# Seven-product pairs of a ConvFFN: weight sums by adding transfers and VectorE, products reordered over four PSUM banks

## The chip, the cores and the metric

The kernel runs on one core of a Trainium2 chip, as one program of 25725 instructions. The metric is device time in microseconds (us), from the first to the last instruction of the slowest core, here the only one. The core has five engines with a queue each: TensorE (PE, matrix products; its weight loads are listed as PEld), VectorE (DVE), ScalarE (ACT), GpSimd (POOL) and SyncE (SP, which only issues DMAs here). POOL issues DMAs as well; those can add to what lies at their destination.

## The reference

One inference step of a two-layer decoder trunk over 544 tokens (512 of a prompt and 32 of eight samples), model width 1024. Layer 0 mixes tokens by causal pooling, layer 1 by a gated linear recurrence (HGRN2). Each layer ends with the same gated ConvFFN, and the change lies there:

```python
def conv_ffn(h, ctx, w_up, conv_w, conv_b, w_down):
    u = h @ w_up                                   # 1024 -> 2 x 2816
    full = jnp.concatenate([ctx, u], axis=1)
    c = conv_b + sum(full[:, j:j + L] * conv_w[j] for j in range(3))
    gate, val = jnp.split(c, 2, axis=-1)
    y = (jax.nn.gelu(gate, approximate=True) * val) @ w_down   # 2816 -> 1024
    return y, full[:, -2:]
```

All of it is in 32-bit floats. The kernel makes each product out of three faster ones: an operand is split into a rounded high part and the rest (`wh`, `wl` for weights, `xh`, `xl` for activations), and high times high, high times low and low times high are added in PSUM.

## The kernel before

**Tiling.** Activations lie transposed, 128 features by 544 tokens in a tile. `w_up` is cut into 44 blocks of 1024 by 128: 22 of the gate half, 22 of the value half. A pair is gate block j with value block j; its result is 2 x 128 features for 544 tokens. `w_down` is cut along its 2816 rows into five parts (`PARTS`, 6, 4, 4, 3 and 5 blocks of 128), and the output tiles of a part are made once its pairs are done.

**Two ways to make a pair.** The first six pairs of a layer (`SEVEN = PARTS[0]`) are made plainly, by `group` and `block`. The other 16 pairs, j = 6 to 21, are made by `seven(j)` with seven block products in place of eight (Strassen's scheme in Winograd's form): the four quarters are the two halves of the inner dimension by the two blocks of the pair for the weights, and by the two halves of the tokens (`U`, 272 each) for the activations. One product q is 4 k-tiles by 3 partial products, 12 matmuls of 272 columns. It needs sums of weight quarters (`seventh(i, q)`, once per pair) and sums of activation quarters (`operands(k, out)`, once per layer), and afterwards sums of the products on DVE and ACT (the list `after` in `seven`).

**Weight sums before.** `seventh` loads both 1024 by 128 blocks into two `raw` tiles A_ and B_ (512 KB each, three such buffers) and has POOL make three sums when q is 0 and a fourth when q is 6. `ensure_units` then turns each of the seven quarters into `wh` on ACT and `wl` on DVE, in the order of use, up to nine units ahead of the product (`ahead_units`). With the quarters named A.lo, A.hi, B.lo, B.hi the order of use is: sum, A.lo, sum, B.lo, A.hi, B.hi, sum.

**Products before.** Three banks per pair, out of four of the tag `pa`: Y, X, Z, and the seven products go to Y, X, Z, Y, X, Z, Y, of which the fifth and the seventh add to what the bank holds and the fourth and sixth start it anew, once its first value has been read.

**Activation sums.** `operands(k, out)` runs for k = 0 to 3 beside the pairs 4 and 5: two DVE multiplications by the norm's scale, four POOL subtractions of 272 columns, then a split by ACT and DVE (`both`). The results are the right-hand sides of all sixteen pairs.

**Order of the work.** Nothing is issued in program order. All operations are recorded (`Plan.record`) and `emit` makes a list schedule: an instruction's cost comes from `Plan.cost`, DMAs from a small model with a due time, tile buffers are handed out in their order, and each engine's queue is written out in the planned order of start. The engines then run these fixed queues in order, waiting on semaphores. Hence a number in `cost` can change the order on every engine in the whole kernel. `plan.hold` and `plan.after` give the operation recorded next an additional predecessor.

**Convolution buffers.** `new_u(j)` takes a buffer of the tag `t` (22 in all), has POOL clear two columns and copy 16 columns of context into it; DVE or ACT write the block's result beside it; `conv` then has POOL copy the new context out (`cv`, `pv`), ACT make the first tap and DVE the other two; `finish` adds the GELU on ACT and the product of gate and value on DVE, whose split results `yh`, `yl` the down products read.

**Order of pairs and down products.** `MIX` interleaves them: in part 1 the pairs are followed by 4, 4, 0 and 0 down products, in part 2 by 3, 3, 2 and 0, in part 3 by 3, 3 and 2, in part 4 by 2, 2, 2, 2 and 0.

Of the kernel before, what the change touches and what calls it, by code (L numbers as in the profile page):

```python
# [11 lines left out]
F32 = _mybir.dt.float32  # L12
F32R = _mybir.dt.float32r
I32 = _mybir.dt.int32
AF = _mybir.ActivationFunctionType
ALU = _mybir.AluOpType

P = 128
# [58 lines left out]
class Plan:  # L77
# [86 lines left out]
    def cost(eng, name, args, kw):  # L164
# [14 lines left out]
        if name == "dma_start":  # L179
            return 0.475 if eng == "SP" else 1.04  # L180
        ins = [a for a in list(args[1:]) + list(kw.values()) if hasattr(a, "shape")]
# [4 lines left out]
        if eng == "DVE":  # L186
            if name == "memset":
                return 0.01 + n / 960
            return 0.069 + n / (1920 if name == "tensor_scalar" and not psum else 960) + 0.06 * cols
        return 0.13 + n / 475  # L190

    def emit(self):
# [7 lines left out]
        for bufs, keys in self.tags.values():  # L200
            for q in range(bufs, len(keys)):
                extra[self.tiles[keys[q]][1][0]] += self.tiles[keys[q - bufs]][1]
        dma = lambda o: 2.0 + int(np.prod(o[3][0].shape)) * 4 / 359e3
        dur = [o[7] + (dma(o) if o[2] == "dma_start" else 0) for o in ops]
# [51 lines left out]
        for _ in range(n):  # L256
# [31 lines left out]
            if o[2] == "dma_start":  # L288
                st = max(at + o[7] + 0.65, dma_free)
                dma_free = st + dma(o) - 2.0  # L290
                end[i] = dma_free + 0.91
            else:
                end[i] = free[e]
# [52 lines left out]
def trunk_step(ctx: ExitStack, tc: _tile.TileContext, xT, xp, xs, spool, s0, fctx, par, gb0, cst, bands,  # L346
# [91 lines left out]
    raws, casts = {}, {}  # L438
    sums, mine = {}, {}

# [38 lines left out]
    def seventh(i, q):  # L479


        H = 4 * P
        if q == 0:
            raws[i] = A_, B_ = [wp.tile([P, KT * P], F32, tag="raw", name="raw") for _ in range(2)]
            for t, src in zip((A_, B_), stream[i][0]):
                SP.dma_start(t, src)

            mine[i] = dict(sums) or {q: tt((P, H)) for q in range(2)}
            POOL.tensor_tensor(mine[i][0], A_[:, 0:H], B_[:, 0:H], op=ALU.add)
            POOL.tensor_tensor(B_[:, 0:H], B_[:, 0:H], B_[:, H:2 * H], op=ALU.add)  # L490
            POOL.tensor_tensor(mine[i][1], B_[:, 0:H], A_[:, 0:H], op=ALU.add)
        A_, B_ = raws[i]
        if q == 6:
            POOL.tensor_tensor(A_[:, H:2 * H], A_[:, H:2 * H], mine[i][1], op=ALU.add)
        return (mine[i][1], A_[:, 0:H], mine[i][0], B_[:, 0:H], A_[:, H:2 * H], B_[:, H:2 * H], A_[:, H:2 * H])[q]

# [415 lines left out]
    def ffn(li, XH, XL, res, enter, mtag, leave, n_ahead, homes, hv=HV):  # L912
# [14 lines left out]

        def new_u(j):
            u = tt((P, UW))
            us = u[:, 2 + SEQ:UW].rearrange("p (b c) -> p b c", c=6)  # L930
            if li == 0 and j % NPAIR < 8:
                plan.hold(hx[1][64:64 + NS, :])
            POOL.memset(u[:, 0:2], 0.0)
            POOL.tensor_copy(us[:, :, 0:2], cv[:, j])
            return u, us
# [73 lines left out]
        def operands(k, out):  # L1009
# [3 lines left out]
            for z, f in ((za, k), (zb, k + 4)):  # L1013
                DVE.scalar_tensor_tensor(z, x_of(f), pcol(gn + f), R, op0=ALU.mult, op1=ALU.mult)
                SP.dma_start(yT[:, f], x_of(f))
            POOL.tensor_tensor(w[:, U[0]], za[:, U[1]], zb[:, U[1]], op=ALU.subtract)
            POOL.tensor_tensor(w[:, U[1]], za[:, U[0]], za[:, U[1]], op=ALU.subtract)
            POOL.tensor_tensor(za[:, U[1]], za[:, U[0]], w[:, U[0]], op=ALU.subtract)
            POOL.tensor_tensor(s_, zb[:, U[0]], za[:, U[1]], op=ALU.subtract)
            both(out["a", k], za)  # L1020
# [11 lines left out]
        def operand(q, k):  # L1032

            t, c = ((out["a", k], 1), (out["a", k], 0), (out["w", k], 0), (out["w", k], 1), (out["z", k], 0), (out["s", k // 2], k % 2),
                    (out["z", k], 1))[q]
            return t[0][:, U[c]], t[1][:, U[c]]

        def seven(j):
            i = up_i[li, j]
            banks = [ps1()[:, 0:HT] for _ in range(3)]  # L1040
            w, us_ = tt(), {}
            n1 = SEQ - HT

            def u_of(o):
                if o not in us_:
                    us_[o] = new_u(o * NPAIR + j)
                return us_[o]

            def second(o, op, a, b):
# [3 lines left out]
                                  b[:, n1:HT].rearrange("p (b t) -> p b t", t=NL), op=op)  # L1053
            Y, X, Z = banks
            c, t = w[:, U[0]], w[:, U[1]]
            after = (lambda: ACT.activation(c, Y, AF.Identity),
                     lambda: DVE.tensor_tensor(t, c, X, op=ALU.subtract),
                     lambda: DVE.tensor_tensor(c, t, Z, op=ALU.add),
                     lambda: second(1, ALU.subtract, c, Y),
                     lambda: ACT.activation(u_of(0)[0][:, 2:2 + HT], X, AF.Identity),  # L1060
                     lambda: DVE.tensor_tensor(u_of(1)[0][:, 2:2 + HT], c, Z, op=ALU.add),
                     lambda: second(0, ALU.subtract, Y, t))
            for q, (o, more) in enumerate(((Y, 0), (X, 0), (Z, 0), (Y, 0), (X, 1), (Z, 0), (Y, 1))):
                ahead_units(unit0[i] + q)
# [30 lines left out]
        def up(j):  # L1095
# [3 lines left out]
            for b in (j, NPAIR + j):  # L1099
                i = up_i[li, b]  # L1100
                ahead_units(unit0[i])
                t = block(i, rH, rL, KT, HP)
                u, us = new_u(b)
                evac_full(u, us, t)
                finish(u, us, b)
# [639 lines left out]
```

## Time and profile before

| what | us |
|---|---|
| three runs | 1221.56, 1222.04, 1215.65; median 1221.56 |
| the profiled execution | 1218.57 |
| its span, first to last instruction | 1216.7 |
| PE busy | 1157.7 |
| DVE busy | 963.7 |
| ACT busy | 632.7 |
| POOL busy | 475.1 |
| layer 0's ConvFFN after its first pairs | about 100 to 452 of the span |
| layer 1's ConvFFN after its first pairs | about 828 to 1192 of the span |

How to read it: a row of the view of stretches gives, for each engine, its busy time and the number of its instructions in that stretch, then the clock that was granted to TensorE as a share of full speed, the share of the DMA engines that was busy, and GB/s. A row of the grouped view gives line, engine, operation, output<-inputs, shapes and count, then busy time and mean ns of one, then the idle time just before these instructions and who ended it. A row of the timeline gives start, duration, engine, operation, and in brackets the idle time before it and its releaser. A matmul's listed duration (some 290 ns) overlaps with its neighbours', so the number of matmuls in a stretch tells more than their busy time. All planned operations are issued from line 312, so operations are told apart by their tiles: `raw`, `fst`, `sums` and `hold` on POOL are the sums in question (`fst` and `sums` are the places where two of the weight sums are kept), `op`, `k` and `xl` hold the split activation sums, `pa` is the banks' tag.

### The profile page before, as it was taken

The page shows a single profiled execution, that of the slowest core. Times are in us where ns is not written, and L with a number is a line of the kernel's source. Part 1 is how long each engine was busy: PE and PEld are TensorE (multiplying, and loading weights), DVE is VectorE, ACT ScalarE, POOL GpSimd, SP SyncE. Part 2 cuts the span into 40 slices and gives each one's busy share as a digit, 9 for nine tenths or more (in the row PEclk, how much of TensorE's full clock was granted, in tenths as well). Part 3 has the DMA queues.
Part 4 walks back from the last instruction along what each step waited for, and adds up shares of the span by engine and source line. Part 5 has one row for each costly group of instructions (what it writes and reads, how often), then busy time and mean ns, then how long its engine had stood idle before and what let it go on. Part 6 is the DMA issues. An engine that isn't in the chain of part 4 may idle for free.

```text
span 1216.7 us, 25725 instructions
## 1 busy us (share of the span) xinstructions
PE 1157.7 (95%) x9892; PEld 1116.1 (92%) x9892; DVE 963.7 (79%) x2075; ACT 632.7 (52%) x1343; POOL 475.1 (39%) x709
## 2 busy tenths in 40 slices
PE   8999898999999999999999999999899999999895
PEld 7799898998999997999999999999899899998895
DVE  6788776888988877588778985577976998888866
ACT  4665555444444466556555554545545544444552
POOL 3547535354454233111111130427625446355413
PEclk9999999999999999999999999999899999999998
DMA  9883232221321376423232223457141232223232
GB/s 322 188 206 73 61 109 88 88 87 61 113 96 65 110 247 142 105 82 108 92 105 84 83 98 117 119 141 157 40 139 71 71 104 96 78 83 96 63 142 74
DMA packets 55243, 134.04 MB, mean 110 GB/s; under 512 B 6730, under 2 KB 13258, under 8 KB 55112
## 3 DMA queue, kind: packets, MB, share of 16 engines
q1 hardware_dynamic: 37168, 95.90, 23.4%
q0 software_dynamic: 17808, 36.44, 13.0%
q8 instruction: 78, 1.28, 0.4%
q14 instruction: 45, 0.37, 0.1%
q10 hardware_dynamic: 144, 0.05, 0.0%
HBM read 119.96 MB, written 12.77 MB: 109 GB/s over the span
## 4 chain that ended last, share of the span: by engine, by line
PE 58%; DVE 23%; issue 7%; ACT 6%; POOL 4%; DMA 2%; DVEq 0%; SPq 0%; ACTq 0%; POOLq 0%
PE ps L312 30%; PE pa L312 27%; DVE t L312 13%; DVE wl L312 5%; ACT t L312 3%; DVE m L312 2%; ACT wh L312 2%; PE pr L312 2%; POOL raw L312 1%; POOL fst L312 1%; DMA t<-bands 1%; DVE k L312 1%; DVE op L312 1%; POOL wh L312 0%; DMA k<-wup 0%
## 5 line engine op out<-in xcount | busy, mean ns | idle before, releaser
L312 PE MATMUL pa<-op,wh 128*128 128x272 f32 x1152 | 268.8, 298 | 23.6 <-ACT t L312 15.6
L312 ACT ACTIVATE wh<-raw 128x512 fp32r<-128x512 f32 (+2 forms) x294 | 172.7, 597 | 168.6 <-PE ps L312 68.0
L312 PE MATMUL ps<-t,wh 128*128 128x272 f32 x1248 | 241.3, 291 | 6.1 <-ACT t L312 4.2
L312 DVE TENSOR_TENSOR wl<-raw,wh 128x512 fp32r<-128x512 f32 (+2 forms) x294 | 199.5, 691 | 59.4 <-ACT wh L312 53.1
L312 PEld LDWEIGHTS pa<-op,wh 128*128 128x128 f32 x1152 | 200.3, 195 | 29.5 <-ACT t L312 18.9
L312 PE MATMUL pa<-op,wl 128*128 128x272 f32 x768 | 226.3, 295 | 0.9 <-DVE wl L312 0.9
L312 DVE SCALAR_TENSOR_TENSOR t<-t,prm 128x560 f32<-128x560 f32 (+1 forms) x184 | 191.3, 1071 | 22.5 <-ACT t L312 21.7
L312 PEld LDWEIGHTS ps<-t,wh 128*128 128x128 f32 x1248 | 198.1, 190 | 8.2 <-ACT t L312 5.1
L312 DVE TENSOR_TENSOR t<-t 128x512 f32<-128x512 f32 (+10 forms) x332 | 154.3, 487 | 36.4 <-ACT t L312 28.0
L312 PE MATMUL ps<-t,wl 128*128 128x272 f32 x624 | 180.2, 290 | 1.6 <-DVE wl L312 1.6
L312 POOL COPY fst<-t 128x2 f32<-128x2 f32 (+1 forms) x176 | 82.8, 554 | 248.9 <-DVE t L312 248.8
L312 PE MATMUL ps<-xh,wh 128*128 128x256 f32 (+1 forms) x560 | 166.4, 298 | 0.0
L312 ACT ACTIVATE t<-t 128x544 fp32r<-128x544 f32 (+5 forms) x145 | 85.2, 598 | 155.1 <-DVE t L312 152.7
L312 PE MATMUL ps<-xl,wh 128*128 128x256 f32 (+1 forms) x560 | 162.3, 290 | 0.5 <-DVE xl L312 0.5
L312 PE MATMUL ps<-xh,wl 128*128 128x256 f32 (+1 forms) x560 | 160.9, 288 | 0.4 <-DMA wl<-wup 0.4
L312 PEld LDWEIGHTS pa<-op,wl 128*128 128x128 f32 x768 | 149.6, 195 | 1.1 <-DVE wl L312 1.1
L312 PE MATMUL pa<-k,wh 128*128 128x272 f32 (+2 forms) x560 | 139.5, 293 | 4.6 <-ACT k L312 3.4
L312 PEld LDWEIGHTS ps<-t,wl 128*128 128x128 f32 x624 | 118.6, 190 | 2.0 <-DVE wl L312 2.0
L312 PEld LDWEIGHTS ps<-xh,wh 128*128 128x128 f32 x560 | 105.4, 188 | 3.8 <-issue 1.6
L312 PEld LDWEIGHTS ps<-xl,wh 128*128 128x128 f32 x560 | 105.5, 188 | 3.7 <-issue 2.0
L312 PEld LDWEIGHTS ps<-xh,wl 128*128 128x128 f32 x560 | 105.3, 188 | 2.7 <-issue 1.8
L312 PEld LDWEIGHTS pa<-k,wh 128*128 128x128 f32 x560 | 99.4, 192 | 5.4 <-ACT k L312 3.6
(207 smaller groups left out, 2472.7 us busy)
## 6 DMA issues: line engine op xcount, KB each, us to landing
raw<-wup SPq DMA_DIRECT2D x69, 512.0 KB, 3.3
raw<-win SPq DMA_DIRECT2D x26, 512.0 KB, 3.3
wh<-wup POOLq DMA_DIRECT2D x34, 256.0 KB, 5.4
wl<-wup POOLq DMA_DIRECT2D x34, 256.0 KB, 5.0
t<-wdn SPq DMA_DIRECT2D x32, 256.0 KB, 4.1
raw<-wdn SPq DMA_DIRECT2D x16, 384.0 KB, 3.0
raw<-wdn SPq DMA_DIRECT2D x16, 320.0 KB, 4.4
yT<-x SPq DMA_DIRECT2D x16, 272.0 KB, 6.2
```

Of the source, the lines that this page charges most:

```text
L312: o[1](*o[3], **o[4])
```

## The change

`seventh` makes no sum on POOL any more. Two of the four sums are made by DMA: SP loads one quarter into half of B_, and a DMA issued from POOL adds another quarter to it (`accum_op`). DVE makes the other two, in place, when q is 2 and 5. The last quarter gets a buffer of its own (C_). A pair now has four SP loads and two POOL transfers, 1792 KB in all, against two loads of 512 KB. The order of B_ and A_ in the buffers' queue is turned round, as is the order of products, so that the first product takes a plain quarter. The products go to four banks: X, Y, W, Z, X, Y, Z, the last three adding. `operands` makes its subtractions on DVE. `new_u` holds its clearing and its copy until a given bank has been written (in the plain blocks of later pairs: their own bank). Three numbers of the planner change: the cost of a POOL DMA issue, of POOL's small copies and clears, and the duration and landing of POOL's DMAs.

```diff
         if name == "dma_start":
-            return 0.475 if eng == "SP" else 1.04
+            return 0.475 if eng == "SP" else 0.9
...
-        return 0.13 + n / 475
+        if name == "tensor_copy":
+            return 0.55
+        return 0.19 if name == "memset" and n < 99 else 0.13 + n / 475
...
-        dma = lambda o: 2.0 + int(np.prod(o[3][0].shape)) * 4 / 359e3
+        dma = lambda o: 2.0 + int(np.prod(o[3][0].shape)) * 4 / 359e3 * (1.75 if "accum_op" in o[4] else 1)
...
-                end[i] = dma_free + 0.91
+                end[i] = dma_free + (2.4 if e == "POOL" else 0.91)
...
     def seventh(i, q):
         H = 4 * P
+        lo, hi = slice(0, H), slice(H, 2 * H)
+        w0, w1 = stream[i][0]
         if q == 0:
-            raws[i] = A_, B_ = [wp.tile([P, KT * P], F32, tag="raw", name="raw") for _ in range(2)]
-            for t, src in zip((A_, B_), stream[i][0]):
-                SP.dma_start(t, src)
-
-            mine[i] = dict(sums) or {q: tt((P, H)) for q in range(2)}
-            POOL.tensor_tensor(mine[i][0], A_[:, 0:H], B_[:, 0:H], op=ALU.add)
-            POOL.tensor_tensor(B_[:, 0:H], B_[:, 0:H], B_[:, H:2 * H], op=ALU.add)
-            POOL.tensor_tensor(mine[i][1], B_[:, 0:H], A_[:, 0:H], op=ALU.add)
-        A_, B_ = raws[i]
-        if q == 6:
-            POOL.tensor_tensor(A_[:, H:2 * H], A_[:, H:2 * H], mine[i][1], op=ALU.add)
-        return (mine[i][1], A_[:, 0:H], mine[i][0], B_[:, 0:H], A_[:, H:2 * H], B_[:, H:2 * H], A_[:, H:2 * H])[q]
+            B_, A_ = [wp.tile([P, KT * P], F32, tag="raw", name="raw") for _ in range(2)]
+            raws[i] = A_, B_, sums[i % 2] if sums else tt((P, H))
+            SP.dma_start(B_[:, hi], w1[:, lo])
+            POOL.dma_start(B_[:, hi], w1[:, hi], accum_op=ALU.add)
+            SP.dma_start(A_, w0)
+            SP.dma_start(B_[:, lo], w0[:, lo])
+            POOL.dma_start(B_[:, lo], w1[:, lo], accum_op=ALU.add)
+            SP.dma_start(raws[i][2], w1[:, hi])
+        A_, B_, C_ = raws[i]
+        if q in (2, 5):
+            DVE.tensor_tensor(B_[:, hi], B_[:, hi], A_[:, lo if q == 2 else hi], op=ALU.add)
+        return (A_[:, lo], B_[:, hi], B_[:, hi], B_[:, lo], A_[:, hi], B_[:, hi], C_)[q]
...
-        def new_u(j):
+        def new_u(j, bank=None):
...
+            if bank is not None:
+                plan.after(bank)
             POOL.memset(u[:, 0:2], 0.0)
+            if bank is not None:
+                plan.after(bank)
             POOL.tensor_copy(us[:, :, 0:2], cv[:, j])
...
-            POOL.tensor_tensor(w[:, U[0]], za[:, U[1]], zb[:, U[1]], op=ALU.subtract)
+            DVE.tensor_tensor(w[:, U[0]], za[:, U[1]], zb[:, U[1]], op=ALU.subtract)
...
-            banks = [ps1()[:, 0:HT] for _ in range(3)]
+            banks = [ps1()[:, 0:HT] for _ in range(4)]
...
-                    us_[o] = new_u(o * NPAIR + j)
+                    us_[o] = new_u(o * NPAIR + j, X)
...
-            Y, X, Z = banks
+            X, Y, W, Z = banks
             c, t = w[:, U[0]], w[:, U[1]]
-            after = (lambda: ACT.activation(c, Y, AF.Identity),
-                     lambda: DVE.tensor_tensor(t, c, X, op=ALU.subtract),
-                     lambda: DVE.tensor_tensor(c, t, Z, op=ALU.add),
-                     lambda: second(1, ALU.subtract, c, Y),
+            after = (lambda: ACT.activation(c, X, AF.Identity),
+                     lambda: None,
+                     lambda: (DVE.tensor_tensor(t, W, c, op=ALU.subtract), DVE.tensor_tensor(c, t, Y, op=ALU.subtract)),
+                     lambda: second(1, ALU.add, c, Z),
                      lambda: ACT.activation(u_of(0)[0][:, 2:2 + HT], X, AF.Identity),
-                     lambda: DVE.tensor_tensor(u_of(1)[0][:, 2:2 + HT], c, Z, op=ALU.add),
-                     lambda: second(0, ALU.subtract, Y, t))
-            for q, (o, more) in enumerate(((Y, 0), (X, 0), (Z, 0), (Y, 0), (X, 1), (Z, 0), (Y, 1))):
+                     lambda: second(0, ALU.subtract, Y, t),
+                     lambda: DVE.tensor_tensor(u_of(1)[0][:, 2:2 + HT], t, Z, op=ALU.add))
+            for q, (o, more) in enumerate(((X, 0), (Y, 0), (W, 0), (Z, 0), (X, 1), (Y, 1), (Z, 1))):
...
-                u, us = new_u(b)
+                u, us = new_u(b, None if li == 0 and j < 8 else t[:, 0, 0:HP])
```

The other three subtractions of `operands` move from POOL to DVE in the same way, and `operand(q, k)` names the activation quarters in the new order.

More of the change, by code (lines that the diff above doesn't have):

```diff
@@ L438, in trunk_step @@
     raws, casts = {}, {}
-    sums, mine = {}, {}
+    sums = {}
     def ensure(upto):
@@ L1015, in operands @@
                 SP.dma_start(yT[:, f], x_of(f))
-            POOL.tensor_tensor(w[:, U[0]], za[:, U[1]], zb[:, U[1]], op=ALU.subtract)
-            POOL.tensor_tensor(w[:, U[1]], za[:, U[0]], za[:, U[1]], op=ALU.subtract)
-            POOL.tensor_tensor(za[:, U[1]], za[:, U[0]], w[:, U[0]], op=ALU.subtract)
-            POOL.tensor_tensor(s_, zb[:, U[0]], za[:, U[1]], op=ALU.subtract)
+            DVE.tensor_tensor(w[:, U[0]], za[:, U[1]], zb[:, U[1]], op=ALU.subtract)
+            DVE.tensor_tensor(w[:, U[1]], za[:, U[0]], za[:, U[1]], op=ALU.subtract)
+            DVE.tensor_tensor(za[:, U[1]], za[:, U[0]], w[:, U[0]], op=ALU.subtract)
+            DVE.tensor_tensor(s_, zb[:, U[0]], za[:, U[1]], op=ALU.subtract)
             both(out["a", k], za)
@@ L1032, in operand @@
         def operand(q, k):
-            t, c = ((out["a", k], 1), (out["a", k], 0), (out["w", k], 0), (out["w", k], 1), (out["z", k], 0), (out["s", k // 2], k % 2),
-                    (out["z", k], 1))[q]
+            t, c = ((out["a", k], 0), (out["w", k], 1), (out["a", k], 1), (out["w", k], 0), (out["z", k], 0),
+                    (out["z", k], 1), (out["s", k // 2], k % 2))[q]
             return t[0][:, U[c]], t[1][:, U[c]]
```

## The prediction

> **What bounds the kernel now.** I read the page's engine lines first, then stretches, waits and the timeline of one wait.
>
> ```profile
> span 1216.7 us, 25725 instructions
> PE 1157.7 (95%) x9892; PEld 1116.1 (92%) x9892; DVE 963.7 (79%) x2075; ACT 632.7 (52%) x1343; POOL 475.1 (39%) x709
> ```
>
> PE is the bound, so an edit is worth only the PE time it frees. How much can be freed is read from stretches of the two ConvFFNs:
>
> ```profile
> core 0: us, PE busy (x) PEld busy (x) DVE busy (x) ACT busy (x) POOL busy (x), PEclk, DMA share, GB/s
> 100.00:141.00 41.00, 37.24 (x281) 36.44 (x280) 38.07 (x58) 22.33 (x39) 26.66 (x38) 0.96 0.22 56
> 187.00:452.00 265.00, 250.72 (x1910) 247.29 (x1909) 223.25 (x378) 134.02 (x242) 114.13 (x167) 0.97 0.31 102
> 864.00:885.00 21.00, 15.86 (x102) 14.87 (x102) 20.50 (x31) 12.69 (x23) 11.36 (x14) 0.84 0.14 49
> 885.00:930.00 45.00, 45.00 (x360) 44.88 (x359) 29.05 (x51) 22.14 (x40) 17.35 (x21) 1.00 0.34 106
> 930.00:1157.00 227.00, 212.88 (x1624) 208.75 (x1624) 196.32 (x318) 108.89 (x195) 110.85 (x154) 0.98 0.25 84
> ```
>
> At 885 to 930 PE runs undisturbed: 360 matmuls in 45 us, 0.125 us each. At that pace the other rows would need 35.1, 238.8, 12.8 and 203.0 us; they take 41, 265, 21 and 227. So 5.9 + 26.2 + 8.2 + 24.0 = 64.3 us are lost: 14.1 where the activation sums are made, 50.2 among the sixteen pairs of each layer. Undisturbed, DVE is busy 29.05 of 45 us (65%); in the lossy rows 223.25 and 196.32 us against 238.8 and 203.0 of PE work (93% and 97%). DVE is nearly a second bound there. Why it is:
>
> ```profile
> L312 DVE SCALAR_TENSOR_TENSOR t<-t,prm 128x560 f32<-128x560 f32 x56 | 65.7, 1211 | 7.6 <-ACT t L312 7.5
> L312 DVE TENSOR_TENSOR wl<-raw,wh 128x512 fp32r<-128x512 f32 x75 | 53.9, 731 | 12.9 <-ACT wh L312 12.5
> L312 DVE SCALAR_TENSOR_TENSOR t<-t,prm 128x560 f32<-128x560 f32 x52 | 60.8, 1212 | 6.0 <-ACT t L312 5.9
> L312 DVE TENSOR_TENSOR wl<-raw,wh 128x512 fp32r<-128x512 f32 x66 | 48.0, 743 | 13.3 <-ACT wh L312 13.1
> ```
>
> These are groups of 187 to 452 (two rows) and of 930 to 1157; the next fence has the timeline of one wait, by engine.
>
> ```profile
> 1101.97 1.67 POOL L312 TENSOR_TENSOR raw<-raw 128x512 f32<-128x512 f32 x1
> 1103.72 1.68 POOL L312 TENSOR_TENSOR fst<-raw 128x512 f32<-128x512 f32 x1
> 1103.05 2.95 DVE L312 SCALAR_TENSOR_TENSOR t<-t,prm 128x560 f32<-128x560 f32 x2
> 1106.55 0.79 DVE L312 SCALAR_TENSOR_TENSOR t<-t,prm 128x560 f32<-128x560 f32 x1
> 1109.44 0.68 DVE L312 TENSOR_TENSOR wl<-fst,wh 128x512 fp32r<-128x512 f32 x1
> 1110.04 0.43 DVE L312 TENSOR_TENSOR t<-t,pa 128x272 f32<-128x272 f32 x1
> 1106.03 0.68 ACT L312 ACTIVATE t<-t 128x560 f32<-128x560 f32 x1 [3.98 <-DVE t L312]
> 1108.99 0.37 ACT L312 ACTIVATE t<-pa 128x272 f32<-128x272 f32 x1
> 1109.42 0.52 PE L312 MATMUL pa<-op,wh 128*128 128x272 f32 x2 [1.90 <-ACT t L312]
> ```
>
> A convolution tap takes 0.79 us alone; the two that lie over POOL's weight sums take 2.95 together, though all these operands differ. ACT, in order, waits 3.98 us for the taps (the GELU); behind that GELU stand five casts and then the reading of the first bank (t<-pa, at 1108.99), and PE cannot start the fourth product over that bank: 1.90 us. PE's waits of this kind:
>
> ```profile
> PE pa L312 <- ACT t L312: 7.1, 5, 2.2
> PE pa L312 <- ACT t L312: 8.4, 6, 1.9
> ```
>
> (187 to 452, then 930 to 1157): 15.5 us in 11 waits, and more by the clock after them, seen after the wait of 2.2 us that ends at 369.9:
>
> ```profile
> 363.00:370.00 7.00, 4.80 (x39) 4.58 (x37) 6.90 (x10) 3.50 (x8) 2.79 (x2) 1.00 0.13 44
> 370.00:373.00 3.00, 3.00 (x17) 3.00 (x18) 2.93 (x8) 1.54 (x3) 0.32 (x1) 0.65 0.00 0
> 373.00:375.00 2.00, 2.00 (x13) 2.00 (x12) 1.55 (x3) 0.38 (x1) 1.91 (x3) 0.67 0.00 0
> ```
>
> The granted clock falls to 0.65 and 30 matmuls take 5 us in place of 3.75. Over the two long stretches clocks of 0.97 and 0.98 make 265 x 0.03 + 227 x 0.02 = 12.5 us of the 50.2.
>
> **The change, part by part.**
>
> *POOL's weight sums go; two adds per pair come to DVE.* The first long stretch has 56 taps, 4 a pair, so 14 pairs; by the same count the second has 13 (52 taps). Above the undisturbed 0.79 and 0.68, the 56 taps lose 56 x 0.42 = 23.5 us and the 75 splits 75 x 0.05 = 3.8: 27.3 us, about 2 a pair. In the second, 52 x 0.42 + 66 x 0.06 = 25.8. A 128x512 add costs the 0.60 between the starts at 1109.44 and 1110.04; two are 1.2 a pair, 16.8 us. DVE's work falls from 223 to 223.25 - 27.3 + 16.8 = 212.8, or 89% of PE's; in the second, with 25.8 off and 15.6 on, from 97% to 92%. Where does that take PE's loss? From 0 at 65% to 26.2/238.8 = 11.0% at 93%, a straight line gives 9.3% at 89% (22.2 us) and some 10.3% at 92% (20.9): a gain of 4 + 3 us. That is the low end, as load alone counts; it misses that taps no longer double, unforeseen by the fixed order.
>
> *The chain of sums goes.* Two pairs without down products between them show it:
>
> ```profile
> 197.47 1.30 POOL L312 TENSOR_TENSOR sums<-raw 128x512 f32<-128x512 f32 x1 [2.93 <-ACT t L312]
> 198.84 1.67 POOL L312 TENSOR_TENSOR raw<-raw 128x512 f32<-128x512 f32 x1
> 200.58 1.67 POOL L312 TENSOR_TENSOR fst<-raw 128x512 f32<-128x512 f32 x1
> 202.29 0.63 ACT L312 ACTIVATE wh<-fst 128x512 fp32r<-128x512 f32 x1 [3.22 <-POOL fst L312]
> ```
>
> 4.8 us from landed weights to the first cast. Now the first product takes a quarter as loaded. Late next is A_'s own load, whose buffer comes free at the pair before's sixth cast:
>
> ```profile
> raw<-wup SPq DMA_DIRECT2D x69, 512.0 KB, 3.3
> wl<-wup POOLq DMA_DIRECT2D x34, 256.0 KB, 5.0
> L312 POOL DMA_DIRECT2D wl<-wup x34 | 30.6, 981 | 21.3 <-ACT wl L312 21.2
> ```
>
> 3.3 us, which two products (24 x 0.125 = 3.0) and the casts' lead cover nearly. I count 3.5 saved once per layer, 7 (bounds 0 and 9.6).
>
> *Four banks.* The fourth product starts a fresh bank; the first bank's reading is needed at the fifth, one product (12 x 0.125 = 1.5 us) later. The 11 waits average 1.4, the longest is 2.2: most vanish even if ACT is as late as now. Of 15.5 us, two waits belong to the chain above (about 2 each); of the other 11.5 I take 9 (bounds 4 and 11.5). With them goes about half of the 12.5 us of slow clock: 6 (bounds 1 and 11). Each reuse still has two products of slack, except the next pair's first bank, read by ACT after the fifth product and needed after the seventh: 3 us, where the old order gave the next pair's second product one product.
>
> [...]
>
> *Adding transfers.* Per pair 768 KB more move, and two issues of 0.98 us stand on POOL in place of four sums of 1.3 to 1.7. DMA is 0.31 busy at 102 GB/s; 14 x 0.79 MB in 240 us add 46 GB/s, well under the 322 GB/s of the page's first slice, so 0:
>
> ```profile
> GB/s 322 188 206 73 61 109 88 88 87 61 113 96 65 110 247 142 105 82 108 92 105 84 83 98 117 119 141 157 40 139 71 71 104 96 78 83 96 63 142 74
> ```
>
> Latency: 3.3 + 5.0 us through both transfers, plus split (0.6 + 0.7), is about 9.6 before the second product. B_ goes into the buffer that the pair before the last left, at least one pair of 84 matmuls (10.5 us) and two products (3.0) ahead: covered by 4 us. If that cover is gone, each late landing costs PE its whole delay (rival below). Each adding transfer also waits in POOL's queue for SP's landing; behind it stand the copies and clears of the convolution buffers, for which ACT's first tap waits, then DVE's taps. The wait is up to 3.3 us and the new buffers are not needed before a pair ends: 0, bounds -1 and +1.5 us a pair.
>
> *Activation sums on DVE.* The chain into the first seven-product pair:
>
> ```profile
> 120.51 2.60 POOL hold L312 x3
> 123.94 1.23 POOL hold L312
> 125.17 1.23 POOL t L312
> ```
>
> 5.1 us of the path are POOL's. DVE's price for 272 columns lies between 0.43 (the row with pa at 1110.04) and the tap's 0.79; I take 0.43: the four of one k are 1.7. But DVE is busy 38.07 of 41 and 20.50 of 21 us there, and takes on 16 x 0.43 = 6.9 us a layer while the taps shrink. So of the 14.1 lost I count 4.5 (bounds 0 and 8).
>
> *Held buffers, planner's numbers.* The copy into a new buffer now waits for the bank, with DVE's reading of that bank (0.43) beside it as cover:
>
> ```profile
> L312 POOL COPY t<-fst 128x16 f32<-128x16 f32 x88 | 35.0, 426 | 11.4 <-DMA fst<-fctx 5.7 <-PE pr L312 5.7
> ```
>
> 0.43 beside 0.43 costs 0; without the cover 0.4 a block for the first tap, none of it PE's while a down product runs. The planner's numbers issue no instruction, yet every queue is ordered anew. PE's idle time outside the five stretches is 1216.7 - 1157.7 - 37.3 = 21.7 us; a quarter of that either way, +-5, is my estimate of the bounds; I take 0.
>
> **Sum:** 7 + 9 + 6 + 4.5 = 26.5 us off the profiled execution's 1218.57: 1192. The median of the three runs, 1221.56, is 3 above that execution; the forecast is for a run like the profiled one.
>
> **The rivals.**
>
> - *DVE stays the bound.* Load alone, 89 to 92%, sets PE's loss: 4 + 3 from the line above and 4.5 at the entry leave 1207. For it: 38.07 of 41 busy at the entry, where PE loses just as much with few sums about. Against it: the waits named go through doubled taps. 20%.
> - *The order fits at last.* With every DVE duration as planned, three quarters of the 64.3 us go, as the stretch at 885 has no loss at all: 1218.57 - 48 = 1170. For it: the waits recur at the same places of both layers. Against it: DVE at 92%. 13%.
> - *A new wait takes the place.* A_'s load begins only at the sixth cast; where the lead of casts is short, all pairs, not only adjacent ones, wait: 3.3 and 1.3 of split less the 3.0 of two products is 1.6, of which casts made ahead cover half; 32 x 0.8 = 26 cancels the gain: 1218. 10%.
> - *Slower: POOL's queue behind landings.* If adding transfers land later than the 4 us of cover allow (the median is 5.0, but that is with POOL free to issue), second and fourth products wait. At 1.5 us a pair, 48 us less the 26.5 gained: 1240. It decides from a chain over 13.5 us, free buffer to split; below that it costs nothing. Against it: 3.3 + 5.0 + 1.3 is 9.6. 12%.
>
> **How the numbers follow.** Forecast 1192, 45% (1183 to 1202 by itself). About 0.5%, some 6 us, is what a measurement here tells from no change, so faster means under 1215.5 against the median: forecast, the first two rivals, 78%. Same 10%, slower 12%. The range 1170 to 1220 takes in the terms' bounds (all low: 0 + 4 + 1 + 0, 1214; all high: 9.6 + 11.5 + 11 + 8, 1178) with the planner's 5 either way, and the first three rivals but for half of the second; it leaves out the slower one.
>
> **What would show it.** Right: taps of 0.79 in the pairs' stretches, matmul counts nearer to 8 per us there, a granted clock of 0.99, no ACT t wait before a fourth product, POOL's busy time down by more than 100 us. Wrong: PE waits on wh or wl whose releaser is a DMA or POOL's queue; taps still over 1 us though no sums run on POOL; DVE with no gap and PE still short of 8 per us.

## The result, and the profile after

The changed kernel takes 1171.43 us (median of four runs, 1170.7 to 1172.7), the one before 1218.61 us beside it: a ratio of 0.9613, 95% interval 0.9577 to 0.965. The forecast was 1192 within 1170 to 1220. Direction and range held; the gain is 47 us and not the 26.5 of the sum.

The page of the kernel after, cut to the rows that answer to those of before (engines; chain; the convolution's taps; DMA issues, with KB each and us to landing):

```profile
span 1168.9 us, 25943 instructions
...
PE 1145.5 (98%) x9896; PEld 1103.7 (94%) x9896; DVE 931.6 (80%) x2171; ACT 643.7 (55%) x1343; POOL 324.1 (28%) x613
...
PE 92%; DVE 4%; DMA 1%; ACT 1%; issue 1%; SPq 0%; DVEq 0%; ACTq 0%
...
L314 DVE SCALAR_TENSOR_TENSOR t<-t,prm 128x560 f32<-128x560 f32 (+1 forms) x184 | 141.2, 795 | 2.4 <-ACT t L314 1.7
...
raw<-wup SPq DMA_DIRECT2D x64, 256.0 KB, 3.5
raw<-wup POOLq DMA_DIRECT2D x64, 256.0 KB, 5.7
```

The same chain line of the page before, by engine:

```profile
PE 58%; DVE 23%; issue 7%; ACT 6%; POOL 4%; DMA 2%; DVEq 0%; SPq 0%; ACTq 0%; POOLq 0%
```

Now 92% of the chain that ends last is PE, where 58% was; POOL is busy 151 us less, and a tap takes 0.795 us. Next the view of stretches of the kernel after: the entry to the seven-product pairs of layer 0, its pairs, all that lies between the ConvFFNs, then entry and pairs of layer 1:

```profile
core 0: us, PE busy (x) PEld busy (x) DVE busy (x) ACT busy (x) POOL busy (x), PEclk, DMA share, GB/s
117.00:149.00 32.00, 32.00 (x258) 32.00 (x257) 29.13 (x58) 19.25 (x34) 9.91 (x18) 1.00 0.32 89
149.00:410.00 261.00, 261.00 (x2080) 261.00 (x2079) 222.73 (x430) 146.91 (x254) 66.79 (x151) 1.00 0.56 153
410.00:835.00 425.00, 419.65 (x4167) 392.99 (x4166) 320.90 (x920) 239.02 (x616) 106.52 (x160) 1.00 0.41 115
835.00:854.00 19.00, 19.00 (x153) 19.00 (x153) 17.77 (x35) 12.67 (x25) 6.41 (x15) 1.00 0.12 43
854.00:1116.00 262.00, 262.00 (x2090) 262.00 (x2089) 221.74 (x420) 142.36 (x246) 66.94 (x152) 1.00 0.53 143
```

In four of the five rows PE has no gap at all: 2080 matmuls in 261.00 us are 0.1255 us each, at a clock of 1.00. The 64 us that the prediction found lost in these stretches are gone, entries and pairs alike. The middle row went the other way; before, that stretch took 416 us:

```profile
438.00:854.00 416.00, 412.15 (x4166) 391.34 (x4166) 311.73 (x896) 236.20 (x611) 109.16 (x174) 1.00 0.41 113
```

The balance by matmul number (from the times of all matmuls in both traces, without the filler products of the tile `wz`; the stretches start at the 750th, 1000th, 3080th, 7250th, 7400th and 9480th): the four FFN stretches take 64.0 us less, the part ahead of them 4.5 more, the part between them 9.0 more, what follows 0.4 more, and the outgoing transfers after the last computing instruction 2.3 more. 64.0 - 16.2 = 47.8, the difference of the spans. So two things want an explanation: why all of the loss went and not 26 us of it, and why some 16 us were lost where the change touches nothing.

PE's waits over the whole kernel after (us in total, times, longest):

```profile
PE pr L314 <- DVE t L314: 3.3, 2, 2.3
PE ps L314 <- DVE t L314: 2.3, 1, 2.3
PE pa L314 <- DVE q L314: 2.0, 2, 1.6
PE pa L314 <- DVE t L314: 1.4, 3, 0.5
```

No wait of `pa` on ACT's `t` is left, nor any on `wh` or `wl`.

### The profile page after: what moved, and what is told of

Same layout as the page of the kernel before. It is cut to its first block, busy times and chain, and to the rows that moved or that the text cites. A ratio compares the mean times of both kernels' runs of the same rounds, so it can differ in the third digit from the quotient of the medians.

```text
span 1168.9 us, 25943 instructions
## 1 busy us (share of the span) xinstructions
PE 1145.5 (98%) x9896; PEld 1103.7 (94%) x9896; DVE 931.6 (80%) x2171; ACT 643.7 (55%) x1343; POOL 324.1 (28%) x613
## 4 chain that ended last, share of the span: by engine, by line
PE 92%; DVE 4%; DMA 1%; ACT 1%; issue 1%; SPq 0%; DVEq 0%; ACTq 0%
PE pa L314 46%; PE ps L314 44%; PE pr L314 3%; DVE t L314 2%; DVE m L314 1%; DMA t<-pw 1%; ACT t L314 1%; DMA k<-xp 1%; DVE o L314 0%; DVE wl L314 0%; DVE x L314 0%; DVE c L314 0%; SPq L314 0%; DVE Al L314 0%; DVE q L314 0%
## 5 line engine op out<-in xcount | busy, mean ns | idle before, releaser
L314 ACT ACTIVATE wh<-raw 128x512 fp32r<-128x512 f32 x326 | 192.3, 602 | 196.5 <-PE ps L314 78.0
L314 DVE TENSOR_TENSOR wl<-raw,wh 128x512 fp32r<-128x512 f32 x326 | 211.3, 661 | 67.3 <-ACT wh L314 58.3
L314 PE MATMUL pa<-op,wh 128*128 128x272 f32 x1152 | 255.8, 288 | 0.0
L314 PE MATMUL ps<-t,wh 128*128 128x272 f32 x1248 | 236.6, 288 | 0.0
L314 PE MATMUL pa<-op,wl 128*128 128x272 f32 x768 | 221.6, 289 | 0.0
L314 PEld LDWEIGHTS pa<-op,wh 128*128 128x128 f32 x1152 | 193.2, 189 | 0.0
L314 POOL COPY fst<-t 128x16 f32<-128x16 f32 (+1 forms) x176 | 95.8, 611 | 322.2 <-DVE t L314 322.2
L314 DVE TENSOR_TENSOR t<-t 128x512 f32<-128x512 f32 (+9 forms) x332 | 141.3, 448 | 24.5 <-ACT t L314 18.0
L314 PEld LDWEIGHTS pa<-op,wl 128*128 128x128 f32 x768 | 144.6, 188 | 0.0
L314 DVE SCALAR_TENSOR_TENSOR t<-t,prm 128x560 f32<-128x560 f32 (+1 forms) x184 | 141.2, 795 | 2.4 <-ACT t L314 1.7
```

What stands on the lines that cost most here:

```text
L314: o[1](*o[3], **o[4])
```

## The experiments

"Loss" below is the time between the first matmuls of two stretches less 0.1255 us for each matmul between them, entries and pairs of both layers added up; "tap" is the mean `SCALAR_TENSOR_TENSOR` of 560 columns in the pairs of layer 1; "ACT on DVE" is the time that ACT waits for DVE's `t` (the convolution's results) in the pairs of layer 0. Each ratio is against runs of the kernel before on the same chip.

| run | median us | ratio (95%) | loss entries | loss pairs | tap us | ACT on DVE us |
|---|---|---|---|---|---|---|
| before | 1218.6 | 1 | 15.0 | 49.5 | 1.19 | 76 |
| numbers_only | 1213.0 | 0.9945 (0.9923 to 0.9967) | 15.4 | 40.6 | 1.23 | 67 |
| four_banks | 1212.8 | 0.9944 (0.9924 to 0.9963) | 16.6 | 42.5 | 1.18 | 77 |
| sums_on_dve | 1208.1 | 0.9899 (0.9869 to 0.993) | 20.9 | 33.9 | 0.80 | 70 |
| transfers_only | 1207.6 | 0.9896 (0.9873 to 0.9919) | 19.7 | 30.0 | 0.80 | 56 |
| transfers_four_banks | 1205.7 | 0.9888 (0.9853 to 0.9922) | 12.4 | 32.8 | 0.80 | 73 |
| dve_sums_four_banks | 1196.1 | 0.9806 (0.9782 to 0.9831) | 15.0 | 24.7 | 0.80 | 79 |
| two_sums_back | 1180.2 | 0.9674 (0.9636 to 0.9713) | -0.1 | 12.5 | 0.85 | 27 |
| subtractions_back | 1178.2 | 0.9662 (0.9639 to 0.9685) | 5.2 | -0.4 | 0.80 | 16 |
| idle_clears | 1171.9 | 0.9608 (0.9572 to 0.9643) | -0.1 | 0.4 | 0.80 | 17 |
| idle_adds | 1215.6 | 0.9981 (0.9957 to 1.0006) | 1.9 | 46.7 | 1.01 | 16 |
| old_numbers | 1164.6 | 0.9542 (0.9511 to 0.9574) | -0.1 | 1.4 | 0.80 | 16 |
| after | 1171.4 | 0.9613 (0.9577 to 0.965) | -0.1 | 0.3 | 0.80 | 17 |
| column_sums | 1153.6 | 0.9458 (0.9426 to 0.949) | -0.1 | -0.5 | 0.80 | 16 |

**One part at a time on the kernel before: numbers, banks, sums.** `numbers_only` puts the four planner numbers of the diff into the kernel before and changes nothing else.

> The kernel before with the planner's new numbers alone (costs of POOL's issues, copies and clears, landing of POOL's DMAs). Collision theory (POOL's sums double DVE's taps, ACT comes late, PE waits): taps still about 1.2 us in the pairs' stretches, within 6 us of before, about 1218. Load theory (DVE's share of PE's work sets PE's loss): the same, as the work is unchanged. Order theory (the new numbers make a queue order that fits the chip): most of the 47 us, under 1190.

`old_numbers` is the reverse: the changed kernel with the planner's numbers of before.

> The changed kernel with the planner's old numbers. Collision and load theory: the pairs' stretches stay free of PE waits, total within 8 us of the changed kernel's 1171. Order theory: over 1195, waits back in the pairs. If the losses outside the pairs (about 14 us against before at matmul 250 to 500, 4500 to 5750 and 6500 to 7000) come from the new numbers, these vanish and the total is about 1158.

The numbers gain 7 us on the kernel before (0.9945) and lose 7 on the kernel after: 1164.6 without them, 1171.4 with them. The gain of the change isn't theirs.

`four_banks` gives the fourth and the seventh product of the kernel before a bank of their own:

```diff
-            banks = [ps1()[:, 0:HT] for _ in range(3)]
+            banks = [ps1()[:, 0:HT] for _ in range(4)]
...
-            Y, X, Z = banks
+            Y, X, Z, V = banks
...
-            for q, (o, more) in enumerate(((Y, 0), (X, 0), (Z, 0), (Y, 0), (X, 1), (Z, 0), (Y, 1))):
+            for q, (o, more) in enumerate(((Y, 0), (X, 0), (Z, 0), (V, 0), (X, 1), (Z, 0), (V, 1))):
```

> The kernel before, its seven products in the old order, but the fourth and seventh in a bank of their own (four banks a pair). Prediction's step: ACT t waits of 15.5 us shrink by 9 and 6 us of slow clock go with them, 1203, with taps still at 1.2 us. If the banks are what holds PE altogether: under 1190. If ACT's lateness only moves to the next product: 1215 to 1220.

6 to 7 us, all of it in the pairs (49.5 to 42.5). `sums_on_dve` moves the four weight sums of the kernel before from POOL to DVE:

```diff
-            POOL.tensor_tensor(mine[i][0], A_[:, 0:H], B_[:, 0:H], op=ALU.add)
+            DVE.tensor_tensor(mine[i][0], A_[:, 0:H], B_[:, 0:H], op=ALU.add)
```

(and the other three alike).

> The kernel before with all four weight sums of a pair on DVE and none on POOL: 4 x 0.6 = 2.4 us a pair more work on DVE, about 2 us of doubled taps less. Collision theory: taps at 0.8 us, PE's loss in the pairs falls well under 50 us although DVE's share stays at 93 to 97%: 1185 to 1200. Load theory: DVE's share is that of before or more, so the loss is too: 1218 to 1226.

The taps fall from 1.19 to 0.80 us at once, and the time by 12 us. So the doubled taps did come from POOL's sums. But of the pairs' 49.5 us of loss 33.9 stay, though no instruction on DVE is stretched any more.

**The price of a collision, by itself.** Both kernels are the kernel after with four more POOL instructions in each pair of layer 1, released by the first product; nothing reads what they write. In one they add two SBUF operands, in the other they only write:

```diff
                 after[q]()
+                if li == 1 and q == 1:
+                    for _ in range(4):
+                        plan.after(X)
+                        POOL.tensor_tensor(A.rearrange("p a b -> p (a b)"), cs[:, 0:512], cs[:, 64:576], op=ALU.add)
```

`idle_clears` has `POOL.memset(A.rearrange("p a b -> p (a b)"), 0.0)` in place of the last line.

> The changed kernel plus four POOL adds of 128x512 a pair in layer 1 alone, two SBUF inputs, output read by nobody, released by the pair's first product. Collision theory: taps in layer 1 rise to about 1.0 to 1.2 us while those of layer 0 stay at 0.8, and PE loses 5 to 15 us in layer 1's pairs: 1176 to 1186. Load theory: no change of taps beyond noise, 1171. Queue theory (POOL's busy queue holds the convolution buffers): loss as with idle_clears.

> As idle_adds, but four POOL memsets of the same 128x512 in place of the adds: POOL writes SBUF and reads nothing. Collision theory, if the shared thing is the reading of SBUF: taps stay at 0.8 in layer 1, 1171 to 1173. If writing collides too: as idle_adds. Queue theory: as idle_adds in proportion to POOL's time.

The adds take back the whole gain, 44 us for 64 of them, three times what was expected at most; the clears cost nothing. DVE's groups in the pairs of layer 1 (count, busy us and mean ns, idle time ahead) with the adds:

```profile
L314 DVE TENSOR_TENSOR wl<-raw,wh 128x512 fp32r<-128x512 f32 x102 | 84.8, 849 | 14.4 <-ACT wh L314 14.4
L314 DVE SCALAR_TENSOR_TENSOR t<-t,prm 128x560 f32<-128x560 f32 x60 | 58.7, 1008 | 0.8 <-ACT t L314 0.7
L314 DVE TENSOR_TENSOR raw<-raw 128x512 f32<-128x512 f32 x30 | 25.0, 834 | 0.2
...
L314 DVE TENSOR_TENSOR m<-m,ps 128x544 f32<-128x544 f32 x24 | 17.1, 714 | 1.8 <-PE ps L314 1.8
L314 DVE TENSOR_TENSOR t<-t 128x32 f32<-128x32 f32 x16 | 13.4, 836 | 0.0
...
L314 DVE TENSOR_TENSOR t<-t,pa 128x272 f32<-128x272 f32 x30 | 12.9, 431 | 2.9 <-PE pa L314 2.3
```

and with the clears:

```profile
L314 DVE TENSOR_TENSOR wl<-raw,wh 128x512 fp32r<-128x512 f32 x102 | 69.0, 687 | 19.2 <-ACT wh L314 18.1
L314 DVE SCALAR_TENSOR_TENSOR t<-t,prm 128x560 f32<-128x560 f32 x60 | 45.9, 796 | 0.8 <-ACT t L314 0.7
L314 DVE TENSOR_TENSOR raw<-raw 128x512 f32<-128x512 f32 x30 | 20.5, 685 | 0.2
L314 DVE TENSOR_TENSOR m<-m,ps 128x544 f32<-128x544 f32 x24 | 17.2, 716 | 3.2 <-PE ps L314 3.2
L314 DVE TENSOR_TENSOR t<-t,pa 128x272 f32<-128x272 f32 x30 | 13.0, 432 | 1.4 <-PE pa L314 1.3
...
L314 DVE TENSOR_TENSOR t<-t 128x32 f32<-128x32 f32 x15 | 2.8, 183 | 0.0
```

With the adds, taps, splits and weight sums, whose two inputs lie in SBUF, grow by 22 to 27% in the mean; the instructions with one input in PSUM don't grow at all (`m<-m,ps`, 714 ns against 716; `t<-t,pa`, 431 against 432). Beside the clears, which read nothing, taps, splits and weight sums take 796, 687 and 685 ns, the same as in the kernel after. So these adds, with two SBUF inputs, stretched the DVE instructions that have two as well, and clears of the same 128x512 left every mean above where it was. The price was not in proportion to the instruction's work: an operation of 32 columns, also with two SBUF inputs, goes from 0.18 to 0.84 us in the mean, while the median tap stays at 0.80 us in both kernels. So at least half of the taps lost nothing, and the longest took 2.32 us, 1.5 above the median. What it costs PE is in the stretch of those pairs, with the adds:

```profile
858.00:1166.00 308.00, 275.09 (x2084) 270.94 (x2083) 281.03 (x424) 137.90 (x246) 162.26 (x214) 0.96 0.46 121
```

DVE is busy 281 us, where PE's work is 2084 x 0.1255 = 261.5: here DVE has more to do than PE. (The adds hold POOL for 1.63 us each and the clears for 0.66, so POOL's own queue differs between the two as well. But in that stretch of `idle_adds` no wait of PE, ACT or DVE is put down to POOL, so its queue is not what costs the time.)

`two_sums_back` gives POOL only the two sums that the change had given to DVE:

```diff
         if q in (2, 5):
-            DVE.tensor_tensor(B_[:, hi], B_[:, hi], A_[:, lo if q == 2 else hi], op=ALU.add)
+            POOL.tensor_tensor(B_[:, hi], B_[:, hi], A_[:, lo if q == 2 else hi], op=ALU.add)
```

> The changed kernel with the two adds that DVE makes (q = 2 and 5) on POOL instead; the adding transfers, the four banks and the order stay. Collision theory: taps that lie over these sums take up to 1.8 us again, mean near 1.0, and PE waits return in part: 1178 to 1195. Load theory: DVE has 1.2 us a pair less to do, so no loss: 1165 to 1172.

1180.2: 9 us lost, 12.5 of loss back in the pairs, taps at 0.82 to 0.85. Half of the sums on POOL, in the new order, cost a quarter of what the pairs had lost.

**What is left without collisions.** `transfers_only` makes the weight sums of the kernel before as the change does (two by adding transfers, two by DVE), with products, banks, numbers and buffers of before (the diff shows the new lines; there the quarter that the list calls B.lo holds B.lo + B.hi when its turn comes, and the first product's sum is that plus A.lo):

```diff
+            SP.dma_start(B_[:, 0:H], w1[:, 0:H])
+            POOL.dma_start(B_[:, 0:H], w1[:, H:2 * H], accum_op=ALU.add)
+            SP.dma_start(A_, w0)
+            SP.dma_start(mine[i][0], w0[:, 0:H])
+            POOL.dma_start(mine[i][0], w1[:, 0:H], accum_op=ALU.add)
+            SP.dma_start(B_[:, H:2 * H], w1[:, H:2 * H])
...
+        if q == 0:
+            DVE.tensor_tensor(mine[i][1], B_[:, 0:H], A_[:, 0:H], op=ALU.add)
...
+            DVE.tensor_tensor(A_[:, H:2 * H], A_[:, H:2 * H], mine[i][1], op=ALU.add)
```

> The kernel before with two of its weight sums by adding transfers and two by DVE, none on POOL; old order of products, three banks, old planner's numbers, subtractions on POOL. If the sums' place is what counts (collision and DVE's load together): taps 0.8 us, PE's loss in the pairs under 10 us of 49, total 1178 to 1190, with the 15 us lost at the two entries kept. If three banks or the old order hold PE by themselves: 20 to 35 us of loss stay in the pairs, 1195 to 1210.

The row of its layer-0 pairs in the view of stretches:

```profile
156.00:432.00 276.00, 266.56 (x2085) 265.10 (x2084) 224.58 (x430) 142.67 (x252) 63.26 (x146) 0.98 0.53 144
```

DVE is busy 224.58 us, as in the kernel after (222.73); the taps take 0.80; and PE still needs 276 us for what the kernel after does in 261. The load on DVE is therefore not what sets PE's loss. `dve_sums_four_banks` (sums_on_dve with the fourth bank) and `transfers_four_banks` (transfers_only with the fourth bank) ask whether it is the banks:

> The kernel before with its four weight sums on DVE (as in sums_on_dve, which lost 34 us in the pairs, taps at 0.8 us and DVE busy 92% of PE's work) and a bank of its own for the fourth and seventh product (as in four_banks). If three banks made that loss: under 15 us of it stays, 1188 to 1195. If DVE's load makes it: 25 to 40 us stay, 1203 to 1210.

> The kernel before with the weight sums as in the change (two by adding transfers, two by VectorE) and a fourth bank for the fourth and seventh product, but with the products, their operands, the planner's numbers and the buffers as before, so that the first product still takes a quarter that VectorE has to add. It tells the banks from the order of the products in what transfers_only left (14.7 and 15.3 us of PE loss among the pairs, 9.5 and 10.2 at the entries). Theory 'banks': the rest is the reuse of the first bank; with the fourth the pairs' loss falls from 30 us to under 8, and the time from 1207.6 to some 1183 to 1187. Theory 'order of the products': the rest is the chain from the transfers through VectorE's add to the first product's cast; the banks take only the waits on ACT t (16.3 us by their rows, of which the two sevens that stand back to back keep their part), 15 to 28 us of loss stay among the pairs, and the time is 1192 to 1205. In both the taps take 0.80 us, VectorE is busy about 85% of PE's work, and the entries keep 15 us or more of loss.

With DVE's sums the bank gains 12 us (1208.1 to 1196.1, and 24.7 us of loss in the pairs, between the two forecasts), with the transfers 2, which is within the intervals of the two ratios (1207.6 to 1205.7): the pairs' loss stays there, 30.0 before and 32.8 after it. The theory "banks" falls, with 45 of the kernel before's 64.5 us still lost. Where they are, the timeline of one wait in `transfers_four_banks` shows, ACT and DVE first, then PE:

```profile
203.02 0.63 ACT L312 ACTIVATE wh<-fst 128x512 fp32r<-128x512 f32 x1 [5.15 <-DVE fst L312]
...
209.55 0.63 ACT L312 ACTIVATE wh<-raw 128x512 fp32r<-128x512 f32 x1 [1.80 <-DVE raw L312]
210.19 1.28 ACT L312 ACT_TABLE_LOAD   x1
211.49 0.67 ACT L312 ACTIVATE t<-t 128x560 f32<-128x560 f32 x1
213.02 0.66 ACT L312 ACTIVATE t<-t 128x544 fp32r<-128x544 f32 x1 [0.86 <-DVE t L312]
213.58 0.38 ACT L312 ACTIVATE t<-pa 128x272 f32<-128x272 f32 x1
```

```profile
202.23 0.69 DVE L312 TENSOR_TENSOR fst<-raw 128x512 f32<-128x512 f32 x1 [2.81 <-DMA raw<-wup]
```

```profile
214.02 0.82 PE L312 MATMUL pa<-k,wh 128*128 128x272 f32 x2 [7.55 <-ACT t L312]
```

DVE waits for a landing and makes the sum `fst` for the next pair's first product. That landing is not an adding transfer's, which had come at 192.95; it is A_'s own load, issued at 196.98, when the pair before had left the buffer. ACT, whose queue is fixed, waits 5.15 us for that sum. Behind it stand casts and two taps, then the cast of the pair's last sum, for which ACT waits another 1.80 us, then the table load, the GELU and a wait of 0.86 us for DVE's product behind it; only at 213.58 does it read the bank, and PE has waited 7.55 us for that. A fourth bank only moves the point at which this reading is needed; the reading itself is seven microseconds late, because weight sums stand ahead of it. The same wait is in `dve_sums_four_banks`, which has no adding transfer:

```profile
213.27 0.59 PE L312 MATMUL pa<-k,wh 128*128 128x272 f32 x1 [6.60 <-ACT t L312]
```

There ACT waits 3.78 us for DVE's `t`, which stands behind a weight sum in DVE's queue, and 2.23 us for the pair's last sum. The four longest waits of PE among the pairs of `transfers_four_banks` (7.55, 5.34, 2.04 and 2.04 us) all lie where one pair follows another with no down product between. ACT's waits in the pairs of layer 0 (us in total, times, longest), first `transfers_four_banks`, then before, then after:

```profile
ACT t L312 <- DVE t L312: 72.6, 40, 4.7
...
ACT wh L312 <- DVE fst L312: 13.2, 5, 5.2
```

```profile
ACT t L312 <- DVE t L312: 76.1, 34, 4.3
```

```profile
ACT wh L314 <- DVE raw L314: 21.5, 19, 2.6
ACT t L314 <- DVE t L314: 16.5, 20, 2.0
```

In all seven kernels with the old order of quarters and products, before among them, ACT waits 56 to 79 us on DVE's convolution there; in all with the new order and no POOL sums in those pairs it waits 16 to 17. In the kernel after ACT still waits 21.5 us for DVE's weight sums, but in pauses of 2.6 us at most, and none of them reaches PE.

`transfers_four_banks` and `dve_sums_four_banks` differ only in who makes the sums, and the one with less work on DVE is 9.5 us slower. ACT's waits on `fst` are 13.2 us against 4.8 in the pairs of layer 0. For the first two pairs of each layer the landing that DVE waits for ahead of `fst` is an adding transfer's (at 152.3 and 173.3, 884.7 and 908.4), for the next two it is A_'s plain load. How much of the 9.5 us is the adding transfers' no run tells. In the kernel after the first product takes a plain quarter and waits for neither sum.

Between `transfers_four_banks` and the kernel after lie the order of quarters and products (and with it the order of A_ and B_ in the buffers' queue, and a place for the last quarter that alternates from pair to pair), DVE's activation subtractions, the held buffers and the numbers. Two of these were taken out of the kernel after: the numbers in `old_numbers` above, and the subtractions in `subtractions_back`, the kernel after with the four subtractions of `operands` on POOL:

```diff
-            DVE.tensor_tensor(w[:, U[0]], za[:, U[1]], zb[:, U[1]], op=ALU.subtract)
+            POOL.tensor_tensor(w[:, U[0]], za[:, U[1]], zb[:, U[1]], op=ALU.subtract)
```

(and the other three alike).

> The changed kernel with the four subtractions of operands on POOL again; weight sums, banks and order as changed. If POOL's price for them (1.1 to 1.2 us each on the path) makes the 15 us lost at the two entries: loss there comes back, 10 to 15 us, 1181 to 1187. If the weight sums' adds made it: 1171 to 1175, no loss at the entries.

It is 7 us slower, 5.2 of which are loss at the entry to layer 0; at the entry to layer 1 it costs nothing. So some 33 us of the pairs' loss are left for the order of quarters and products, with its buffers, together with the held buffers. Those weren't tried apart, and no run has the new order with three banks. That the order does it is an argument from the timeline above, not something that a run shows by itself.

**What was lost elsewhere.** `colsums` in the kernel before and after sums squares over the partitions with groups of four matmuls of 32 output rows, and makes each of a group wait for one square alone, the one with the highest index:

```python
        for k in ks:
            j = k % 4 * 32
            plan.after(sqs[ks[-1]])
            PE.matmul(pn[j:j + 32], ones[:, 0:32], sqs[k], start=(k < 4), stop=(k >= 4), skip_group_check=True)
```

PE's timeline near the end of the HGRN's stretch, first in the kernel before (each such sum counts twice in x):

```profile
799.52 0.69 PE L312 MATMUL pr<-t,cs 128*32 128x288 f32 x8
800.14 0.39 PE L312 MATMUL ps<-oh,sp 128*128 128x256 f32 x1
```

and in the kernel after:

```profile
776.17 0.67 PE L314 MATMUL pr<-t,cs 128*32 128x288 f32 x2
776.77 0.38 PE L314 MATMUL ps<-k,wh 128*128 128x256 f32 x1
777.00 0.28 PE L314 MATMUL ps<-oh,wl 128*128 128x256 f32 x1
777.20 0.67 PE L314 MATMUL pr<-t,cs 128*32 128x288 f32 x2
```

Four sums side by side take 0.62 us (799.52 to 800.14); one alone takes 0.60 (776.17 to 776.77). If the square with the highest index is not the last to be made, each sum of a group gets ready at another time, and the planner may put other products between them; the names in the trace don't tell the squares apart, so this is read from the code. `column_sums` is the kernel after in which every sum of a group waits for all its squares:

```diff
-            plan.after(sqs[ks[-1]])
+            plan.after(*(sqs[q] for q in ks))
```

> The changed kernel with the four column sums of a group held until all four squares are written, where they are now held for the one with the highest index. The trace of the changed kernel has these matmuls apart (0.55 to 0.6 us each between other products) where before has four together in 0.57. If that is what the changed kernel loses outside the pairs: 1157 to 1165, groups of four again. If the loss is elsewhere: 1169 to 1173.

1153.6 us, 17.9 less than the kernel after, and the fastest kernel of all: 0.9458 of the kernel before. From the first matmul of each group of `pr<-t,cs` to the next other matmul, the trace has 28.4 us in the kernel after, 19.4 before, and 15.2 here, so 13 of the 17.9 us are the matmuls themselves. The part ahead of the FFN of layer 0, from the first counted matmul on, is back at 101.7 us (before 101.7, after 106.8), the one between the FFNs at 414.8 (416.7 and 425.7). That the numbers of the planner cost 7 us in the kernel after is of a kind with it: `old_numbers` has 104.2 and 421.6 there, and 23.2 us in these groups where the kernel after has 28.4.

## Why the prediction was right, and where it was not

**What bounds, and where.** Right: the loss of the four stretches was the room, and all of it was gained. Taps of 0.80, 2080 matmuls in 261 us, a clock of 1.00, no ACT wait before a fourth product, POOL down by 151 us: each sign that was named came out. But that the time lies in the range, 1.4 us above its lower end, is in part luck: without the 16 us lost elsewhere it would have been some 1155, below the range, where `column_sums` is.

**POOL's sums stretch DVE.** Right, and shown in isolation by `idle_adds` against `idle_clears` (taps of layer 1 at 1.01 against 0.80 us).

**Load alone.** The straight line from DVE's load to PE's loss, and with it the rival "DVE stays the bound" (1207), is wrong. DVE's share fell from 91 to 85% of PE's work (89 and 92% were forecast), and by the line from 0 at 65% to 11% at 93% some 7.9% of 261 us, 20 us a layer, should have stayed. The kernel after loses 0.3 us in both layers, `transfers_only` with the same load 30.0.

**Chain of sums, 7 us.** This is the term that was mis-sized. It was priced as the lateness of one cast at two adjacent pairs in each layer (and its 4.8 us are not from landed weights on, as the prediction reads them: in the row they start from, POOL had waited for ACT's `t`). What the runs show in its place: weight sums stand ahead of the GELU and the reading of a bank in fixed queues, so these are late too. The place was right, as PE's four longest waits in `transfers_four_banks` lie at adjacent pairs, but they are 17 us, with a clock of 0.50 behind the first. Without collisions and with four banks the pairs still lose 32.8 us; with the new order of quarters and products (and its buffers and the held ones) 0.3.

**Four banks and slow clock, 9 + 6 us.** Too large for the banks alone: 7 us on the kernel before, 12 with DVE's sums, 2 with the transfers. The ACT waits that the term counted do not go by the reuse distance alone; they went when ACT was no longer late. Whether the new order would do with three banks was not tried. The slow clock went with them, all of it, where half was counted.

**Activation sums on DVE, 4.5.** The whole loss at the entries went, 15.0 us; the subtractions alone account for 7 of the total (`subtractions_back`).

**Adding transfers, 0.** Right in the kernel after: they land in 5.7 us, 0.7 later than the transfers that the estimate was taken from, and no product waits for them. In the old order of products DVE does wait for them ahead of `fst`, in the first two pairs of each layer (up to 4.65 us). The slower rival's chain of landings exists where a sum comes first.

**Planner's numbers, 0 within 5.** Too narrow: 16.2 us were lost outside the FFN stretches. Part is the numbers (7); 9.0 are in the groups of column sums that the new plan tears apart (19.4 to 28.4 us); the two overlap. `column_sums` gains more than that, 17.9, in part because some of these groups were apart before as well (15.2 us there). The prediction had looked at idle time there, and not at matmuls of which four side by side take 0.62 us and one alone 0.60.

**Held buffers, 0.** Not tried by itself, so it stays open.

Nearest to what happened comes the rival "The order fits at last" (1170). Its time is right by two errors that cancel: it took three quarters of the 64.3 us, all of them went, and 16 were lost elsewhere. Its mechanism is the nearest to what the runs bear out, with one correction: DVE's durations as planned weren't enough (1208). What came with the new order of products, whose first cast needs no sum, was needed too.

## What to carry to other kernels

Ask of each in-order engine what stands behind an instruction that waits for a sum: in `transfers_four_banks` ACT waited 5.15 and 1.80 us for two sums, the reading of a bank was queued behind them, PE waited 7.55 us for that reading, and a bank more did not cure it. Parts of such a change don't add up: on the kernel before no part alone gained more than 12 us, while together they removed 64 us of loss, so price an order of work as a whole and give it a wide range. Where a planner puts the whole program in order, compare the untouched stretches as well, and write the grouping that you rely on into its dependences.

## What the runs showed of the hardware

**Small sums side by side.** Four matmuls of 32 output rows, each to its own quarter of the partitions, took 0.62 us together in the kernel before (799.52 to 800.14) where one took 0.60 in the kernel after (776.17 to 776.77): 3.9 times as many in the same time.

**The clock after short waits.** The granted clock fell after some waits of about 2 us and not after others. In `transfers_four_banks`, stretches that begin where a wait of 7.55, 1.82 and 2.04 us ends:

```profile
214.00:217.90 3.90, 3.88 (x17) 3.88 (x18) 2.31 (x6) 0.00 (x0) 1.16 (x3) 0.50 0.77 242
...
886.00:889.00 3.00, 2.71 (x12) 2.49 (x13) 2.67 (x6) 3.00 (x7) 0.32 (x2) 0.67 0.04 4
1018.10:1020.10 2.00, 1.96 (x15) 1.96 (x16) 1.80 (x5) 0.00 (x0) 0.35 (x3) 1.00 0.79 229
```

```profile
886.09 0.52 PE L312 MATMUL pa<-op,wh 128*128 128x272 f32 x2 [1.82 <-ACT wh L312]
```

```profile
1018.14 0.52 PE L312 MATMUL pa<-op,wh 128*128 128x272 f32 x2 [2.04 <-ACT t L312]
```

In the stretches of the table, over the kernel before, `four_banks`, `transfers_only`, `transfers_four_banks` and `dve_sums_four_banks`, each of the 16 waits of 2.9 us or more was followed by a dozen or more matmuls at about twice the spacing (in the kernel before 0.227 us in place of 0.125 behind the wait that ends at 369.89), and so (eleven or more) were 12 of the 19 waits between 1.5 and 2.7 us. Between 1.5 and 2.7 us the length of a wait alone did not tell what followed: 1.82 us stood ahead of a clock of 0.67, 2.04 us ahead of 1.00. The prediction's rows for its term of the slow clock, 2.2 us ahead of 0.65, are of the same kind.
